# Norm 0's mean eleven ticks sooner, attention's turns and value products two ticks later

## Chip, core and metric

The kernel runs on one core of one Trainium2 chip. Its engines run side by side, each through its own list of instructions: TensorE (PE, with its weight loader PEld), VectorE (DVE), ScalarE (ACT), GpSimd (POOL) and SyncE (SP, which here only issues DMAs). The metric is the device time of one execution in microseconds (us), and lower is better. Single instructions are read from a trace that the hardware profiler took of one execution.

## What is computed

One step of a decoder layer for 1024 prompt tokens and 8 x 8 sample tokens (together T = 1088 columns), width 1024. Cut to the parts that matter here:

```python
proj = rmsnorm(x, norm1_g) @ w_in
q, k, v, glu_a, glu_b, gate_a, gate_b = jnp.split(proj, SPLIT_IDX, axis=-1)
attn = swa(q, k, v, sinks)                      # window 128, 16 heads, 4 key heads
branch_a = attn @ w_o_attn
c = dwconv_valid(glu_a * jax.nn.sigmoid(glu_b), conv_b_w, conv_b_bias)   # 31 taps
branch_b = jax.nn.silu(layernorm(c, ln_b_g, ln_b_b)) @ w_pb
merged = jax.nn.sigmoid(gate_a) * branch_a + jax.nn.sigmoid(gate_b) * branch_b
h = x + merged @ w_out
...
y = h + ffn(rmsnorm(h))                         # up, 3-tap convolution, silu gate, down
```

The layer norm needs, for each token, the mean over the 1024 channels, then the mean of the squares of the centred rows.

## The kernel before

All matrices are held as a high and a low part, so that one product of a weight tile with activations is three matmuls (`mm3`, lines 212 to 214). `stream` multiplies one weight (128 output rows) with all 1088 columns in chunks of 384, 384 and 320, eight inner steps for each chunk, and calls `tick` before each inner step. A **tick** is therefore one group of three products; one weight is 24 ticks.

Other work is woven into these streams. `plan` puts pairs of a due tick and a function on an agenda, sorted by due tick, and `tick` calls those that are due. The function then issues its instructions at this place of the program. The order in which an engine runs them isn't quite the program's: a planner, at build time, goes through all instructions with a model of their durations, and lets each engine take the one of highest priority (earlier in the program, unless `later` shifts it) among those whose inputs it believes ready. The order that comes out is fixed; on the chip each engine follows it and waits where an input isn't there.

**Attention** runs in two halves of the heads (`p` = 0 and 1), beside the streams of gates and convolution branches. A half has eight units of 128 query rows (`attn_unit`) and four sample units (`sample_unit`, steps at ticks 0, 12 and 18). `plan_units` lays units out at a spacing of 22 ticks (first half) or 19 (second), and 13 behind a sample unit; the order is two units, one sample unit, and so on. The first unit's steps that are due at `A_TURN[0]` or later wait for 10 or 16 ticks more. A unit handles two key heads, `g` = 0 and 1:

- `scores(g)` at `A_SCORE`: eight matmuls (L453, L454) into two PSUM banks, copies and masks (L456, L458), then the softmax: maximum (L418), four Exp on ACT (L420), reciprocal (L422), four normalisations on ACT (L424);
- `values()` at tick 8: high and low part of the values;
- `turn(g)` at `A_TURN`: four transposes of the softmax on PE (L465), then a cast on ACT (L247), a subtraction on DVE (L248) and, but for the first unit, a masked copy on DVE (L473), into single buffers `pt` and `pt0`;
- `mix(g)` at `A_MIX`: the product with the values (L484, two or four matmuls of 512 columns), a copy on ACT (L489) and an addition on DVE (L490); for `g` = 1 the result is split (L493, L494 and an accumulating DMA that POOL issues, L495), and in the first half it is written to memory ten ticks on (`attn_spill`).

`turn` moves its evictions 60 priority steps ahead when a branch gate (`gate_u`, Sigmoid, L772) was issued at most three ticks ago.

**The layer norm** over the convolution's output begins in the last of the gate streams (`LAST_GATES`) and goes on beside the attention's output projection (`do_o`). It has four parts (norm 0 to 3, 272 columns each), each with four steps (`ln_steps`) that are due at the ticks in `LN_AT`, counted from the start of the last gate stream: `load` (DMA, L637), `first` (sums over the channels on DVE, L623), `center` and `apply`. `center` issues a product with a matrix of 1/1024 (`mean`, L631, tied behind the last issued product of the streams), the subtraction of its result on DVE (L647), and for each half of the columns a square on ACT (L650) and three additions on DVE (L623). `apply` issues the second mean (L631 too), then square root, reciprocal (L387), scaling (L663) and Silu (L665). `do_o` loads a gate row (`ga`, L1069), runs a Sigmoid on it (L1070) and multiplies each chunk with it (L1074). Evictions of the gates are copies on ACT (L244).

Of the kernel before, what the change touches and what calls it, by code (L numbers as in the profile page):

```python
# [68 lines left out]
FACTOR_AFTER = 1  # L69
A_VALUES = 8  # L70
A_SCORE = (0, 5)
A_TURN = (16, 22)
A_MIX = (23, 29)
SPILL = 10
WEIGHTS_SOONER = -100
THIRD = 6
# [9 lines left out]
W_PARTS = 4  # L86
CONV_LATER = 1200
TURN_SOONER = -60
LN_AT = ((0, 0, 15, 36), (0, 37, 50, 80), (60, 81, 103, 134), (90, 135, 152, 183))
LEAD = (0, 0)  # L90
FIRST_UNIT = (10, 16)
SPACING = ({"u": 22, "s": 13}, {"u": 19, "s": 13})
# [40 lines left out]
class Build:  # L133
# [292 lines left out]
    def attn_unit(self, p, blk, st):  # L426
# [17 lines left out]
        def scores(g):  # L444
            pt = live[g]["pt"] = self.t(self.at, [P, 4, WIN + 4], "p", bufs=2)
            hd = 4 * (2 * p + g)
            nc.gpsimd.tensor_copy(pt[:, :, WIN:WIN + 1], self.c("sink", hd, 4)[:, :, None])
            above = self.masks[:, 0:WIN].bitcast(mybir.dt.uint32)[:, None, :]
            for jj in range(2):
                ps = self.bank("aux").rearrange("p (a b) -> p a b", a=2)  # L450
                for j in range(2):
                    h = 2 * jj + j
                    nc.tensor.matmul(ps[:, j, :], q[g][:, h, qs], kd[g][:, keys], start=True, stop=False)  # L453
                    nc.tensor.matmul(ps[:, j, :], q[g][:, h, qs], kl[g][:, keys], start=False, stop=True)  # L454
                two = pt[:, 2 * jj:2 * jj + 2, 0:WIN]
                nc.scalar.copy(two, ps[:, :, own])  # L456
                other = ps[:, :, 0:WIN] if blk else self.least[:, None, :].to_broadcast([P, 2, WIN])
                nc.vector.copy_predicated(two, above.to_broadcast([P, 2, WIN]), other)  # L458
            self.band_softmax(pt)

        def turn(g):
            pt = live[g]["pt"]
            ps = self.bank("aux")
            for h in range(4):
                nc.tensor.transpose(ps[:, h * P:(h + 1) * P], pt[:, h, 0:P], self.ident)  # L465
            x = self.t(self.at, [P, 2, 512], "pt", F32R)
            parts = [(0, x[:, y]) for y in range(2)]
            with self.later(TURN_SOONER if self.now - self.gated <= 3 else 0):
                self.split_ps(x[:, 0], x[:, 1], ps)
                if blk:  # L470
                    below = self.masks[:, None, WIN:2 * WIN].to_broadcast([P, 8, WIN])
                    x0 = self.t(self.at, [P, 2, 512], "pt0", F32R)
                    nc.vector.tensor_tensor(x0.rearrange("p y (a b) -> p (y a) b", a=4),  # L473
                                            x.bitcast(F32).rearrange("p y (a b) -> p (y a) b", a=4), below, ALU.mult)
                    parts += [(1, x0[:, y]) for y in range(2)]
            live[g]["parts"] = parts

        def mix(g):
            r, o = [slice(x * HD, (x + 1) * HD) for x in (g, 1 - g)]
            av = self.bank("aux")  # L480
            parts = live[g]["parts"]
            for n, (y, x) in enumerate(parts):
                v = vals["vt"][:, y, 2 * g:2 * g + 2, :].rearrange("p x d -> p (x d)")
                nc.tensor.matmul(av, v, x, start=n == 0, stop=n == len(parts) - 1)  # L484
            if g == 0:
                live[0]["t"] = self.t(self.at, [P, 4 * P], "av", bufs=2).rearrange("p (a b) -> p a b", a=4)
            t = live[0]["t"]
            av = av.rearrange("p (a b) -> p a b", a=4)
            nc.scalar.copy(t[r], av[o])  # L489
            nc.vector.tensor_tensor(t[r], av[r], t[r], ALU.add)  # L490
            if g == 1:
                h, l = q[0][:, :, qs], q[1][:, :, qs]
                nc.scalar.copy(h, t)  # L493
                nc.scalar.activation(l, h.bitcast(F32), AF.Identity, scale=-1.0)  # L494
                nc.gpsimd.dma_start(l, t, accum_op=ALU.add)  # L495
                if p == 0:
                    self.plan([(self.now + SPILL, lambda: self.attn_spill(st, qs))])

        steps = [(A_VALUES, values)]
        for g in range(2):  # L500
            steps.append((A_SCORE[g], lambda g=g: scores(g)))
            steps.append((A_TURN[g], lambda g=g: turn(g)))
            steps.append((A_MIX[g], lambda g=g: mix(g)))
        return steps
# [106 lines left out]
    def ln_steps(self, i):  # L611
# [46 lines left out]

        return [(at, f) for at, f in zip(LN_AT[i], (load, first, center, apply))]

# [72 lines left out]
    def phase_x(self):  # L733
# [152 lines left out]
        def plan_units(p):  # L886
# [5 lines left out]
            for kind, n in todo:  # L892
                new = self.attn_unit(p, n, st) if kind == "u" else self.sample_unit(p, n, st)
                wait = 0 if steps else FIRST_UNIT[p]
                steps += [(at + d + wait * (d >= A_TURN[0]), f) for d, f in new]
                at += SPACING[p][kind] + wait
# [1332 lines left out]
```

## Time and profile before

| What | us |
| --- | --- |
| median of three runs | 1634.8 |
| lowest and highest run | 1634.24, 1635.79 |
| the profiled execution | 1633.05 |
| its span, first to last instruction | 1631.3 |
| attention's first half beside the streams | 195 to 370 |
| attention's second half | 440 to 600 |
| last gate stream and norm | 600 to 720 |

A row of a timeline has the start (us from the start of the span), the duration, engine, line, operation and tiles (out<-in) and, in brackets, how long the engine was idle before it and what ended that. Rows of the waits view give who waited for whom, the total in us, how many times, and the longest. In a row of a group, the numbers are minimum, median and maximum in ns, then the first and last start.

### The profile page before, as it was taken

The page shows a single profiled execution, that of the slowest core. Times are in us where ns is not written, and L with a number is a line of the kernel's source. Part 1 is how long each engine was busy: PE and PEld are TensorE (multiplying, and loading weights), DVE is VectorE, ACT ScalarE, POOL GpSimd, SP SyncE. Part 2 cuts the span into 40 slices and gives each one's busy share as a digit, 9 for nine tenths or more (in the row PEclk, how much of TensorE's full clock was granted, in tenths as well). Part 3 has the DMA queues.
Part 4 walks back from the last instruction along what each step waited for, and adds up shares of the span by engine and source line. Part 5 has one row for each costly group of instructions (what it writes and reads, how often), then busy time and mean ns, then how long its engine had stood idle before and what let it go on. Part 6 is the DMA issues. An engine that isn't in the chain of part 4 may idle for free.

```text
span 1631.3 us, 30109 instructions
## 1 busy us (share of the span) xinstructions
PE 1618.2 (99%) x11428; PEld 1602.1 (98%) x11428; DVE 1341.7 (82%) x2395; ACT 911.4 (56%) x1964; POOL 316.2 (19%) x579
## 2 busy tenths in 40 slices
PE   9999999999999999999999999999999999999998
PEld 9999999999999999999999999999999999999997
DVE  7879678999999745788755999988888877989767
ACT  6536387885688755575533466555555555524232
POOL 0211122322132321121003442223232101000000
PEclk9999999999999999999999999999999999999999
DMA  6355455657646576648763532344444325766323
GB/s 212 106 127 129 97 133 117 139 112 154 150 93 130 127 192 227 197 149 219 194 229 101 200 119 84 112 119 115 120 115 117 100 100 163 236 165 160 108 62 110
DMA packets 130585, 229.90 MB, mean 141 GB/s; under 512 B 28552, under 2 KB 78728, under 8 KB 130424
## 3 DMA queue, kind: packets, MB, share of 16 engines
q1 hardware_dynamic: 94872, 140.13, 28.1%
q0 software_dynamic: 35136, 87.45, 23.2%
q8 instruction: 90, 1.47, 0.4%
q14 instruction: 55, 0.45, 0.1%
q10 hardware_dynamic: 432, 0.40, 0.1%
HBM read 157.47 MB, written 64.03 MB: 136 GB/s over the span
## 4 chain that ended last, share of the span: by engine, by line
PE 56%; DVE 2%; DMA 1%; issue 1%; ACT 1%; POOL 0%; POOLq 0%; DVEq 0%; ACTq 0%; SPq 0%
PE mm L212 12%; PE mm L213 12%; PE mm L214 12%; PE aux L214 6%; PE aux L212 6%; PE aux L213 6%; DMA d_ma<-ma 1%; ACT ct L665 0%; DMA ct<-d_c 0%; DMA wraw<-wall 0%; DMA d_t<-ct 0%; DVE ct L673 0%; ACT L665 0%; PE aux L1371 0%; DVE ct L647 0%
## 5 line engine op out<-in xcount | busy, mean ns | idle before, releaser
L212 PE MATMUL mm<-xh,whi 128*128 128x384 f32 (+1 forms) x904 | 299.6, 331 | 0.0
L213 PE MATMUL mm<-xl,whi 128*128 128x384 f32 (+1 forms) x904 | 296.0, 327 | 0.2 <-DVE xl L302 0.2
L214 PE MATMUL mm<-xh,wlo 128*128 128x384 f32 (+1 forms) x904 | 296.2, 328 | 0.0
L213 PEld LDWEIGHTS mm<-xl,whi 128*128 128x128 f32 x904 | 170.1, 188 | 2.4 <-DVE xl L302 0.7
L212 PEld LDWEIGHTS mm<-xh,whi 128*128 128x128 f32 x904 | 170.2, 188 | 1.8 <-ACT xh L301 0.3
L214 PEld LDWEIGHTS mm<-xh,wlo 128*128 128x128 f32 x904 | 169.9, 188 | 0.9 <-DMA wlo<-wall 0.3
L1475 DVE SCALAR_TENSOR_TENSOR acc<-st,fc,acc 128x1104 f32<-128x1104 f32 x88 | 119.9, 1366 | 12.2 <-issue 6.7
L214 PE MATMUL mm<-th,wlo 128*128 128x272 f32 x320 | 92.5, 290 | 0.0
L213 PE MATMUL mm<-tl,wlo 128*128 128x272 f32 x320 | 92.4, 289 | 0.0
L212 PE MATMUL mm<-th,wlo 128*128 128x272 f32 x320 | 92.3, 289 | 0.0
L585 DVE SCALAR_TENSOR_TENSOR bt<-u,consts,bt 128x513 f32<-128x513 f32 x120 | 89.6, 747 | 0.3
L585 DVE SCALAR_TENSOR_TENSOR c<-sm,hsum,c 128x512 f32<-128x512 f32 x120 | 89.4, 745 | 0.1
L214 PE MATMUL mm<-mh,wlo 128*128 128x272 f32 (+4 forms) x304 | 89.0, 293 | 0.0
L585 DVE SCALAR_TENSOR_TENSOR c<-u,consts,c 128x512 f32<-128x512 f32 x112 | 83.5, 746 | 0.3 <-ACT c L596 0.2
L247 ACT CAST whi<-wraw 128x512 fp32r<-128x512 f32 x76 | 47.5, 625 | 63.4 <-DVE wraw L1671 26.4
L1820 ACT COPY st<-mm 128x272 f32<-128x272 f32 (+2 forms) x132 | 43.7, 348 | 55.9 <-PE mm L214 55.9
L247 ACT CAST wlo<-wraw 128x512 fp32r<-128x512 f32 x76 | 47.4, 624 | 40.1 <-DVE wraw L1671 16.5
L1473 ACT ACTIVATE acc<-st,fc 128x1104 f32<-128x1104 f32 x44 | 57.6, 1316 | 15.1 <-DVE st L1776 11.8
L183 ACT CAST whi<-wraw 128x1024 fp32r<-128x1024 f32 x37 | 38.9, 1052 | 47.1 <-PE mm L213 46.0
L212 PE MATMUL aux<-mh,whi 128*128 128x272 f32 (+4 forms) x216 | 63.9, 296 | 0.0
L213 PE MATMUL aux<-ml,whi 128*128 128x272 f32 (+4 forms) x216 | 63.6, 294 | 0.0
L185 POOL DMA_DIRECT2D wlo<-wall x37 | 33.4, 902 | 150.5 <-ACT wlo L184 100.9
(723 smaller groups left out, 5839.1 us busy)
## 6 DMA issues: line engine op xcount, KB each, us to landing
wraw<-wall SPq DMA_DIRECT2D x118, 512.0 KB, 4.0
wlo<-wall POOLq DMA_DIRECT2D x37, 512.0 KB, 6.9
bw<-d_b SPq DMA_DIRECT2D x42, 272.0 KB, 4.0
d_b<-gd POOLq DMA_DIRECT2D x36, 272.0 KB, 6.1
d_b<-acc POOLq DMA_DIRECT2D x24, 272.0 KB, 4.7
ar<-wdn SPq DMA_DIRECT2D x32, 192.0 KB, 4.0
d_g<-acc POOLq DMA_DIRECT2D x10, 544.0 KB, 4.2
ct<-d_c SPq DMA_DIRECT2D x8, 544.0 KB, 6.2
```

The lines of the kernel that those rows point to most:

```text
L183: self.cast = self.nc.scalar.copy(h, r).ins
L185: self.nc.gpsimd.dma_start(l, self.a["wall"][i], accum_op=ALU.add)
L212: mm(ps, wh, xh, start=first, stop=False, skip_group_check=more)
L213: mm(ps, wh, xl, start=False, stop=False, skip_group_check=more)
L214: self.last_mm = mm(ps, wl, xh, start=False, stop=last, skip_group_check=more).ins
L247: self.cast = self.nc.scalar.copy(h, src).ins
L585: mac = lambda o, x, w: nc.vector.scalar_tensor_tensor(o, x, w, o, ALU.mult, ALU.add)
L1473: nc.scalar.activation(acc, st[:, 0:AW], AF.Identity, bias=fb(f), scale=fw(f, 0))
L1475: nc.vector.scalar_tensor_tensor(acc, st[:, k:k + AW], fw(f, k), acc, ALU.mult, ALU.add)
L1820: self.evicted = (add if second and n == 0 and j == 1 else op)(d, r(banks[bank, j]))
```

## The change

Three constants. Turns are due two ticks later behind the start of their unit, and so are the products with the values; scores, values and sample units keep their ticks, and so does the spacing of units. In the first norm part, `center` is due at tick 4 of the last gate stream and no longer at tick 15; `load`, `first` and `apply` stay.

```diff
-A_TURN = (16, 22)
-A_MIX = (23, 29)
+A_TURN = (18, 24)
+A_MIX = (25, 31)
...
-LN_AT = ((0, 0, 15, 36), (0, 37, 50, 80), (60, 81, 103, 134), (90, 135, 152, 183))
+LN_AT = ((0, 0, 4, 36), (0, 37, 50, 80), (60, 81, 103, 134), (90, 135, 152, 183))
```

## The prediction

> **What bounds the kernel now.** I read the page first, then the waits of TensorE (PE), then busy time by stage, then the timelines around each wait.
>
> ```profile
> span 1631.3 us, 30109 instructions
> ...
> PE 1618.2 (99%) x11428; PEld 1602.1 (98%) x11428; DVE 1341.7 (82%) x2395; ACT 911.4 (56%) x1964; POOL 316.2 (19%) x579
> ```
>
> PE is the bound: 13.1 us of 1631.3 are idle. The change removes no PE work, so it can win only idle time, and the places to look at are those that its steps touch. The busy time by stage has the columns stretch, length, then busy us of PE, weight load, DVE, ACT and POOL; the waits view has total, times, longest.
>
> ```profile
> 195.00:370.00 175.00, 173.74 (x1123) 169.23 (x1122) 155.82 (x288) 139.66 (x379) 49.65 (x75) 1.00 0.57 121
> 370.00:440.00 70.00, 70.00 (x429) 69.72 (x428) 68.83 (x113) 37.98 (x71) 10.24 (x16) 1.00 0.66 150
> 440.00:600.00 160.00, 159.15 (x1008) 154.07 (x1007) 133.22 (x257) 127.28 (x367) 46.80 (x69) 1.00 0.55 122
> 600.00:720.00 120.00, 117.63 (x706) 116.17 (x705) 78.67 (x106) 66.10 (x85) 20.44 (x35) 1.00 0.64 210
> ...
> PE aux L631 <- DVE sm L623: 2.4, 2, 2.0
> ...
> PE aux L465 <- ACT p L424: 1.0, 1, 1.0
> PE aux L484 <- DVE pt L248: 0.7, 2, 0.5
> ...
> PE aux L542 <- ACT ts L537: 0.2, 1, 0.2
> ```
>
> The two attention stretches (195 to 370 and 440 to 600) hold 1.26 + 0.85 = 2.1 us of idle PE, the norm stretch 2.4. That is all that the change can win there: 4.5 us, 0.28%. The norm's part is nearly one wait:
>
> ```profile
> 632.85 0.34 PE L213 MATMUL mm<-al,whi 128*128 128x384 f32 x1
> 633.02 0.34 PE L214 MATMUL mm<-ah,wlo 128*128 128x384 f32 x1
> 635.41 0.70 PE L631 MATMUL aux<-sm,mean 128*128 128x272 f32 x2 [2.05 <-DVE sm L623]
> ```
>
> The second mean of norm 0 (the variance, tick 36) waits for the sums of squares. Neighbouring products start 0.17 us apart (632.85, 633.02); here it is 2.39, so the wait costs 2.39 - 0.17 = 2.2 us.
>
> **Norm 0's mean, tick 15 to tick 4.** The chain that makes the sums late:
>
> ```profile
> 616.50 0.34 PE L214 MATMUL mm<-xh,wlo 128*128 128x384 f32 x1
> ...
> 622.39 0.62 PE L631 MATMUL aux<-sm,mean 128*128 128x272 f32 x2
> ...
> 605.39 0.30 DVE L623 TENSOR_TENSOR sm<-u 128x136 f32<-128x136 f32 x1
> ...
> 616.23 1.23 DVE L194 TENSOR_TENSOR wlo<-wraw,whi 128x1024 fp32r<-128x1024 f32 x1 [6.88 <-ACT whi L193]
> 623.05 2.42 DVE L647 TENSOR_TENSOR ct<-ct,aux 128x2176 f32<-128x2176 f32 x1 [5.60 <-PE aux L631]
> 630.65 1.20 DVE L623 TENSOR_TENSOR c<-c 128x544 f32<-128x544 f32 x2 [5.18 <-ACT c L650]
> 631.89 0.30 DVE L623 TENSOR_TENSOR sm<-c 128x136 f32<-128x136 f32 x1
> ...
> 633.73 1.20 DVE L623 TENSOR_TENSOR c<-c 128x544 f32<-128x544 f32 x2
> 634.96 0.30 DVE L623 TENSOR_TENSOR sm<-c 128x136 f32<-128x136 f32 x1
> ...
> 619.52 0.48 ACT L244 COPY gt<-mm 128x384 f32<-128x384 f32 x1 [3.00 <-PE mm L214]
> 626.83 1.28 ACT L1070 ACT_TABLE_LOAD   x1 [6.84 <-DMA ga<-d_ga]
> 628.13 1.12 ACT L1070 ACTIVATE ga<-ga 128x1088 f32<-128x1088 f32 x1
> 629.15 0.46 ACT L244 COPY gt<-mm 128x384 f32<-128x384 f32 x1
> 629.50 1.12 ACT L650 ACTIVATE c<-ct 128x1088 f32<-128x1088 f32 x1
> ```
>
> The centred rows are ready at 623.05 + 2.42 = 625.5, but the first square starts at 629.50: it stands on ACT behind the Sigmoid of the output gate (L1070), which waits 6.84 us for its DMA. So ACT's order makes the sums late. In the last gate stream tick 4 falls after the third group of three products, whose last one starts at 616.50: the mean starts near 616.7, 5.7 us sooner. It adds no PE wait, since its input is done at 605.69, 11 us before. What moves with it: two mean products (0.62), the subtraction (2.42), two squares (1.12 each), six additions (1.50 for each square); no DMA, so no queue of SP or POOL is passed. The subtraction follows L194 on DVE: 617.5 to 619.9. The first square then follows the eviction at 619.52, which the mean in front of it makes 0.6 later: 620.6 to 621.7. Adding up 1.50 with small gaps, the second square, and adding up again (1.1 + 1.5 + 1.1 + 1.5, from 620.6) ends at about 625.9. PE needs it at 633.2. Even if only the second square falls behind the Sigmoid, it starts at about 629.3 and the sums end at 631.9, still in time. Cost of the edit: nothing on PE; **gain 2.2 us**, unless both squares stay behind the Sigmoid. Then the gain is 0. I take 2.2: the planner put the Sigmoid between the evictions at 619.52 and 629.15, and the first square is now ready right behind the first of the two. Next late is the 0.35 that is left of L631's 2.4; I leave it.
>
> **Turns and value products, two ticks later.** A tick is three products, 3 x 0.174 = 0.52 us, so turns stand 1.04 us later behind their softmax. Turn to value product stays seven ticks. No instruction is added. The biggest wait is a turn's:
>
> ```profile
> 339.11 1.28 ACT L772 ACT_TABLE_LOAD   x1
> 340.40 1.06 ACT L772 ACTIVATE u<-u 128x1024 f32<-128x1024 f32 x1
> 341.37 1.26 ACT L424 ACTIVATE p<-p,den 128x128 f32<-128x128 f32 x4
> ...
> 341.80 0.33 PE L465 MATMUL aux<-consts,p 128*128 128x128 f32 x1 [1.03 <-ACT p L424]
> ...
> 467.36 0.73 PE L484 MATMUL aux<-pt,vt 128*128 128x512 f32 x2 [0.54 <-DVE pt L248]
> ```
>
> The turn at 341.80 waits for normalisations that stand on ACT behind the branch gate's table load and Sigmoid. Neither moves. If PE comes 1.04 later, the wait of 1.03 is gone. But counted in groups of products this turn (unit 6 of the first half, due tick 203) already stands two ticks behind its due place: the planner thought its input late. If it stands there again, nothing is won. The row lies between: I take 0.5 of 1.03. What is left of the second stretch's 0.85 beside L484's 0.7, 0.15, I count to the turns too, and all of it goes. Together 0.6. The value products' waits (0.7) and the sample unit's (0.2) hang on evictions and casts whose distance doesn't change; only their neighbours do. I take 0.2 of 0.9. **Sum 0.8 us**, with bounds: 2.1 if all idle time of both stretches goes, and below zero the crowding, next.
>
> What the later steps pass: a first-head value product issues evictions on ACT and DVE only; the second one's also the accumulating DMA on POOL (L495), and in the first half two spills on SP ten ticks on, each also two ticks later. The first half's last spill moves from tick 242 to 244 of the 264 before the second half's queries; the second half's last value product moves from 217 to 219 of 240, and the last sample unit stays behind it at 225. So nothing is cut off, and the loads that follow have room:
>
> ```profile
> 591.15 9.66 SPq L637 DMA_DIRECT2D ct<-d_c  x4
> 600.99 3.29 SPq L1026 DMA_DIRECT2D ah<-d_ah  x1
> ...
> 595.16 1.30 POOL L495 DMA_DIRECT2D q<-av  x1 [1.94 <-ACT q L494]
> ...
> 627.41 0.34 PE L212 MATMUL mm<-ah,whi 128*128 128x384 f32 x1
> ```
>
> If their buffers come free 1.04 us later, the norm's input is at 606.7 instead of 605.7 (needed at 616.7), and ah is issued 25 us before its use. That costs nothing. If this cover were gone, it would cost at most the 1.04. One turn (unit 1, due tick 50) now falls within three ticks of a branch gate and gets its eviction ahead of the gate; one eviction on ACT, inside idle time of ACT (139.66 of 175 busy).
>
> **A reading that gives more.** These rows bear on how much of PE's time is really waiting:
>
> ```profile
> L484 PEld LDWEIGHTS aux<-pt,vt x120: 186/188/228, 223.0 to 590.2; 128*128 128x128 f32 x120
> L484 PE MATMUL aux<-pt,vt x120: 387/395/504, 223.2 to 590.4; 128*128 128x512 f32 x120
> ```
>
> The weight loader is idle for 175 - 169.23 + 160 - 154.07 = 11.7 us in the two stretches, PE for 2.1. Were all of the 11.7 waiting that slack can remove, the gain would be 2.2 + 11.7 = 13.9 us: 1620.9, a rival. The rows speak against it: a value product lasts 395 ns over a load of 188, so its loader pauses although PE works. [...]
>
> **The sum.** -2.2 - 0.8 = -3.0. The profiled execution took 1633.05 us (span 1631.3 and 1.75 around it), so 1630.05 is its own forecast; on the median of 1634.8 it is **1631.8**.
>
> **The rivals.**
> - *The squares stay behind the Sigmoid.* For it: the planner did so before, and fills ACT whenever the gate's load seems landed. Against: the squares are now ready 5.6 us sooner. Time: 1634.8 - 0.8 = 1634.0. [...]
> - *Crowding, slower.* In eight pairs of neighbouring units (four in each half) the second turn now comes two ticks behind the next unit's first scores (spacing 22), or on the very tick of its second scores, with the value product one tick on (spacing 19). Their evictions and softmax meet on ACT and DVE, and the value product or the next turn waits. At the nearest row's 1.03 for each pair that is +8.2, less 2.2: 1640.8. It is slower than before from 0.28 us a pair, and measurably so from 0.68. Against it: the turns gain 1.04 of slack everywhere, and the dense places of before cost 0.5 at most (467.36).
> - *All waits go.* The norm's 2.2 and 0.35, and attention's 2.1: 1630.2.
> - *The change moves nothing that PE feels:* the planner sets every turn and the mean by its own idea of readiness. 1634.8. Against: nearly all turns stand on their due ticks now.
>
> **How the numbers follow.** Forecast 0.60, squares behind the Sigmoid 0.13, crowding 0.10, all waits gone 0.14, no effect 0.02, the weight loads' room 0.01. A difference of about 0.2%, 3.3 us, is what a measurement can tell here; that puts the border of faster at 1631.5, inside the forecast's own range of 1630.6 to 1633.4. Of its 0.60 I put 0.27 below the border, 0.32 within, 0.01 above. Faster: 0.27 + 0.14 + 0.01 = 0.42. Within: 0.32 + 0.13 + 0.02 = 0.47. Slower: 0.01 + 0.10 = 0.11. The range of 1629.9 to 1635.2 takes in the forecast, the Sigmoid case, all waits gone and a crowding of up to 0.3 a pair.
>
> **What would show it.** Norm 0's first mean near 616.7 without idle time before it; both squares ahead of L1070's table load on ACT; no wait of L631 at its second mean, and PE's idle time from 600 to 720 near 0.3. In attention the waits of L465 below 0.6 in all and PE's idle time in the two stretches near 1.3. The prediction is wrong if L650 still follows L1070, or if L465, L484 or L453 show waits of over 2.1 together.

## The result, and the profile after

The changed kernel took 1629.37 us (median of 9 runs, 1628.54 to 1633.16); the kernel before, run again beside it, 1634.24 us (9 runs, 1632.02 to 1635.79). The ratio is 0.9972, with a 95% interval of 0.9963 to 0.9981: faster by 3.1 to 6.0 us. The forecast was 1631.8 and its range ended at 1629.9, so the direction was right and the gain was sized too small. The profiled execution of the changed kernel took 1631.03 us, which is 2.1 us less than the profiled one of before (1633.05), not 4.9: single executions scatter by more than the parts of this change are worth, and that has to be kept in mind below.

The page of the changed kernel, span and busy time:

```profile
span 1629.2 us, 30104 instructions
...
PE 1618.2 (99%) x11428; PEld 1601.7 (98%) x11428; DVE 1342.4 (82%) x2395; ACT 910.8 (56%) x1964; POOL 320.5 (20%) x579
```

PE is busy for the same 1618.2 us as before; the 2.1 us are idle time that went. Where it went shows in busy time by stage (columns as in the prediction):

```profile
195.00:370.00 175.00, 174.95 (x1129) 170.35 (x1129) 156.35 (x289) 139.34 (x379) 47.83 (x75) 1.00 0.57 123
...
440.00:600.00 160.00, 159.16 (x1013) 154.90 (x1012) 132.63 (x257) 126.93 (x365) 51.09 (x70) 1.00 0.56 124
600.00:720.00 120.00, 118.12 (x704) 116.02 (x703) 79.22 (x107) 65.91 (x85) 19.87 (x34) 1.00 0.63 207
```

Attention's first half has 0.05 us of idle PE left, where it had 1.26. The second half still has 0.84, and the norm stretch 1.88 of its 2.37. The waits of PE say why:

```profile
PE aux L631 <- DVE sm L623: 1.7, 1, 1.7
...
PE aux L484 <- DVE pt L248: 0.8, 1, 0.8
```

No turn (L465) waits any more. L631 waits once, and it is another of its instances than before. Norm 0's two means on PE's timeline:

```profile
615.12 0.34 PE L214 MATMUL mm<-xh,wlo 128*128 128x384 f32 x1
615.29 0.62 PE L631 MATMUL aux<-sm,mean 128*128 128x272 f32 x2
...
631.64 0.34 PE L214 MATMUL mm<-ah,wlo 128*128 128x384 f32 x1
631.81 0.62 PE L631 MATMUL aux<-sm,mean 128*128 128x272 f32 x2
```

and the squares on ACT's:

```profile
618.55 1.11 ACT L650 ACTIVATE c<-ct 128x1088 f32<-128x1088 f32 x1 [3.42 <-DVE ct L647]
...
621.32 1.12 ACT L650 ACTIVATE c<-ct 128x1088 f32<-128x1088 f32 x1 [1.29 <-issue]
625.53 1.28 ACT L1070 ACT_TABLE_LOAD   x1 [3.10 <-DMA ga<-d_ga]
```

Both squares now stand ahead of the gate's Sigmoid (L1070), which still waits for its DMA. The second mean follows 0.17 us behind the product in front of it, so it does not wait at all. The wait that L631 has left belongs to norm 2's second mean; here is its row on PE, then DVE's timeline in front of it:

```profile
684.89 0.73 PE L631 MATMUL aux<-sm,mean 128*128 128x272 f32 x2 [1.75 <-DVE sm L623]
...
683.67 0.49 DVE L1074 TENSOR_TENSOR ma<-mm,ga 128x320 f32<-128x320 f32 x1 [2.60 <-DMA d_ma<-ma]
684.07 0.43 DVE L623 TENSOR_TENSOR c<-c 128x272 f32<-128x272 f32 x1
684.54 0.30 DVE L623 TENSOR_TENSOR sm<-c 128x136 f32<-128x136 f32 x1
```

The gated product (L1074) needs one of two buffers `ma`, whose store had not landed, and the norm's last two additions stand behind it.

In attention, what became of the turn that had waited longest (unit 6 of the first half) is on ACT:

```profile
337.69 1.28 ACT L424 ACTIVATE p<-p,den 128x128 f32<-128x128 f32 x4
339.00 1.28 ACT L772 ACT_TABLE_LOAD   x1
340.29 1.21 ACT L772 ACTIVATE u<-u 128x1024 f32<-128x1024 f32 x2
```

and on PE:

```profile
340.91 0.60 PE L465 MATMUL aux<-consts,p 128*128 128x128 f32 x4
```

Before, its four normalisations (L424) stood behind the branch gate's table load and Sigmoid and ended after 342. Now the list of ACT has them ahead, they end at 339.0, and the turn runs on its own due tick, in one piece and without a wait. Counted by products, the 16 turns of the first half stood in 34 pieces before (parts of the last three one to four ticks late, others broken up by products) and stand in 16 pieces now, each on its due tick.

### The profile page after: what moved, and what is told of

It is laid out like the page before. It is cut to its first block, busy times and chain, and to the rows that moved or that the text cites. A ratio compares the mean times of both kernels' runs of the same rounds, so it can differ in the third digit from the quotient of the medians.

```text
span 1629.2 us, 30104 instructions
## 1 busy us (share of the span) xinstructions
PE 1618.2 (99%) x11428; PEld 1601.7 (98%) x11428; DVE 1342.4 (82%) x2395; ACT 910.8 (56%) x1964; POOL 320.5 (20%) x579
## 4 chain that ended last, share of the span: by engine, by line
PE 86%; DVE 7%; DMA 3%; ACT 2%; issue 1%; SPq 0%; DVEq 0%; ACTq 0%; POOLq 0%
PE mm L212 20%; PE mm L213 20%; PE mm L214 20%; PE aux L212 7%; PE aux L213 7%; PE aux L214 7%; DVE c L585 2%; PE aux L484 2%; ACT ct L665 1%; DMA q<-ql 1%; DVE bt L585 1%; PE aux L465 1%; PE aux L453 1%; PE aux L454 1%; DMA ct<-d_c 1%
## 5 line engine op out<-in xcount | busy, mean ns | idle before, releaser
L212 PEld LDWEIGHTS mm<-xh,whi 128*128 128x128 f32 x904 | 170.1, 188 | 1.8 <-ACT xh L301 0.5
```

The lines of the kernel that those rows point to most:

```text
L212: mm(ps, wh, xh, start=first, stop=False, skip_group_check=more)
```

## The experiments

A measure that doesn't depend on what the page calls busy helps to read them. All traces have the same 10,680 products of lines 212 to 214. The table has, for each profiled execution, the time to the start of the 1,201st product (attention begins), and then on to the 2,001st (its first half), the 3,001st (its second half), the 3,601st (norm 0 to norm 2), the 4,601st (next) and the end of the span (rest). The kernel before was profiled four times in all, the changed kernel twice.

| us | to attention | first half | second half | norm | next | rest | span |
| --- | --- | --- | --- | --- | --- | --- | --- |
| before, in the prediction | 200.6 | 176.6 | 207.4 | 107.6 | 136.0 | 803.0 | 1631.3 |
| before_a | 200.2 | 176.7 | 207.2 | 108.5 | 137.7 | 802.1 | 1632.3 |
| before_b | 201.1 | 176.5 | 207.4 | 109.3 | 136.8 | 802.1 | 1633.2 |
| before_c | 200.6 | 176.2 | 207.3 | 108.5 | 137.9 | 802.1 | 1632.7 |
| changed | 200.6 | 175.4 | 207.2 | 107.3 | 136.6 | 802.1 | 1629.2 |
| both_again | 200.5 | 175.4 | 206.4 | 105.8 | 136.8 | 802.1 | 1626.9 |
| norm_alone | 202.9 | 175.4 | 207.1 | 106.2 | 136.4 | 802.1 | 1630.1 |
| turns_alone | 200.7 | 175.4 | 206.2 | 108.3 | 137.5 | 802.1 | 1630.1 |
| norm2_later | 200.7 | 175.4 | 206.5 | 104.7 | 137.5 | 802.9 | 1627.8 |
| centre_10 | 200.9 | 175.4 | 206.0 | 110.1 | 136.4 | 802.1 | 1630.9 |
| third_buffer | 200.5 | 175.4 | 206.0 | 104.9 | 142.3 | 802.4 | 1631.4 |
| turns_4 | 200.5 | 174.6 | 206.2 | 106.5 | 135.4 | 802.4 | 1625.6 |
| turns_sooner | 200.9 | 178.8 | 206.8 | 105.7 | 139.4 | 803.4 | 1635.0 |
| three_together | 200.5 | 174.7 | 206.6 | 104.8 | 142.4 | 802.5 | 1631.5 |

The mean of the four rows of before and the mean of the two of the changed kernel differ by 1.1 us in attention's first half (176.5 and 175.4), 0.5 in the second (207.3 and 206.8), 2.0 in the norm (108.5 and 106.5) and 0.4 in the next stage, most of which the change doesn't touch; the spans by 4.3 (1632.4 and 1628.1).

**both_again**: the changed kernel, unaltered.

> The changed kernel once more, profiled and timed. Theory A (norm 2's second mean waits by chance, for a store that lands late in some executions): the same 4 to 5 us faster than before as in the first timing, and in the new trace the wait of L631 is anything from 0.3 to 1.8 us, not 1.75 again. Theory B (the norm's gain is given back there each time): the wait is 1.75 again within 0.2, and the gain stays 4 to 5 us although the profiled spans differ by 2.1 only, which B can't explain.

Measured: 1628.97 us (6 runs), ratio 0.9971, interval 0.9960 to 0.9983. The gain repeats. The wait at norm 2's second mean was 0.79 us here and 1.75 in the first profile of the same kernel, so its size is a matter of the execution, as theory A has it.

**norm_alone** and **turns_alone**: one part each.

```diff
 norm_alone, against the changed kernel
-A_TURN = (18, 24)
-A_MIX = (25, 31)
+A_TURN = (16, 22)
+A_MIX = (23, 29)
 turns_alone, against the changed kernel
-LN_AT = ((0, 0, 4, 36), ...
+LN_AT = ((0, 0, 15, 36), ...
```

> Only the first norm's mean at tick 4, turns and value products at their old ticks. Theory A: 2.2 us faster than before (ratio 0.9987), both squares ahead of the gate's Sigmoid on ACT, no wait of L631 at its second mean; attention's waits of before (L465 1.0, L484 0.7) stay. Theory B: the same at the second mean, but 1.4 of it come back as a longer wait at norm 2's second mean: 0.5 to 0.8 us faster. Theory C (the two edits act on each other through the planner's order): neither, under 0.3 us.

> Only the turns and value products two ticks later, the norm's mean back at tick 15. Theory A: 1.4 to 2.4 us faster than before, L465 without a wait, the wait of 2.05 of L631 at norm 0's second mean still there. Theory B: 3.5 to 4 us faster, most of the whole. My prediction's size for this part was 0.8.

Measured, beside a kernel before of 1634.27: norm_alone 1631.41, ratio 0.9984 (0.9976 to 0.9993), turns_alone 1632.89, ratio 0.9992 (0.9983 to 1.0000). That is 2.9 us (1.1 to 3.9) and 1.4 us (0 to 2.8), 4.2 together, against 5.3 for both in the same comparison; the intervals are over 1 us wide to each side, so the parts add as far as this can tell. The waits of turns_alone:

```profile
PE aux L631 <- DVE sm L623: 3.1, 2, 2.2
```

The 2.2 at norm 0's second mean is back without the norm's edit, and there is no row of L465. So each edit removes the wait that it was aimed at, and not the other's. Norm 2's wait was 0.90 in turns_alone and 1.16 in norm_alone; it isn't a price of the norm's edit alone.

The table has one surprise: norm_alone's first half takes 175.4 us like that of the changed kernel, though its turns stand at their old ticks. The norm's edit can't be why: up to 610 us PE, ACT and DVE have the same lists as in before, with unit 6's normalisations behind the gate's Sigmoid. But PE, which had reached attention 2.3 us late (it waited 1.0 us near 9, and 1.1 near 180 for a DMA), came to that turn 2.1 us later than in the first profile of before, and the normalisations only 1.2 us later (342.54 and 341.37), so the turn waited 0.13. The whole 1.1 us fall between the 1,801st and the 1,861st product, around this unit's turns. So that is where the first half of before loses this time, and a PE that comes later against ACT gets it back too.

**norm2_later**: is norm 2's wait worth removing by a later second mean?

```diff
-(60, 81, 103, 134)
+(60, 81, 103, 138)
```

> The changed kernel with norm 2's second mean four ticks later (tick 138, not 134), so 2.1 us more room where the changed kernel waited 1.75. Theory A: the wait is gone from the profile, the median gains 0 to 0.7 us over the changed kernel, as the wait is long in few executions only. Theory B: 1.7 us faster than the changed kernel.

Measured: 1631.18, ratio 0.9984 (0.9975 to 0.9993), some 2 us slower than the changed kernel in the same comparison, where theory A forecast a gain of up to 0.7 and theory B one of 1.7. Norm 2's wait is gone from its profile, but norm 3's second mean waits in its place:

```profile
706.87 0.34 PE L214 MATMUL mm<-q,wlo 128*128 128x384 f32 x1
709.12 0.72 PE L631 MATMUL aux<-sm,mean 128*128 128x272 f32 x2 [1.91 <-DVE sm L623]
```

The later step pushes its scaling and Silu into the next part's squares: the Silus start 2.2 us later than in both_again's profile (694.67 and 692.43) and norm 3's second square 1.9 us later (706.04 and 704.10). This profile is of the fastest of its eleven executions (1629.60), so it doesn't show where the 2 us of the median went.

**centre_10**: is it the sooner mean, or the place of the squares on ACT?

```diff
-LN_AT = ((0, 0, 4, 36), ...
+LN_AT = ((0, 0, 10, 36), ...
```

> The changed kernel with norm 0's centring at tick 10 instead of 4 (before it was 15). At tick 10 the list of ACT puts both squares (L650) behind the output gate's Sigmoid (L1070) again, although their mean is still five ticks sooner than before. Theory D (the place of the squares on ACT, ahead of the Sigmoid that waits for its gate row, is what the norm's gain comes from): PE waits again about 2 us (1.5 to 2.5) at norm 0's second mean near 631, the first square again starts right behind the Sigmoid, and the time is that of the turns alone, 1632.9 (1631.8 to 1633.9), or 1631.1 at least. Rival E (a sooner mean is enough, wherever the squares stand): no wait there of over 0.4, and the time of the changed kernel, 1629.2 (1628.2 to 1630.2).

Measured: 1632.59, ratio 0.9997 (0.9988 to 1.0006); nothing is left of the norm's gain. ACT in that profile:

```profile
617.24 0.48 ACT L244 COPY gt<-mm 128x384 f32<-128x384 f32 x1 [3.00 <-PE mm L214]
624.40 1.28 ACT L1070 ACT_TABLE_LOAD   x1 [6.68 <-DMA ga<-d_ga]
625.69 1.11 ACT L1070 ACTIVATE ga<-ga 128x1088 f32<-128x1088 f32 x1
626.71 1.10 ACT L650 ACTIVATE c<-ct 128x1088 f32<-128x1088 f32 x1
```

The subtraction ended at 620.6 (618.17 + 2.42, on DVE), the first square could have run then, and it runs at 626.71, because the Sigmoid stands first and waits for its DMA until 624.40. Theory D holds, and rival E falls: what counts is on which side of the waiting Sigmoid the squares stand. And PE pays more than the wait:

```profile
632.97 0.77 PE L631 MATMUL aux<-sm,mean 128*128 128x272 f32 x2 [1.89 <-DVE sm L623]
633.30 0.75 PE L212 MATMUL mm<-ah,whi 128*128 128x384 f32 x1
633.85 0.52 PE L213 MATMUL mm<-al,whi 128*128 128x384 f32 x1
634.17 0.52 PE L214 MATMUL mm<-ah,wlo 128*128 128x384 f32 x1
```

Behind the wait the products take 0.52 us and start 0.32 apart, where they take 0.34 and start 0.17 apart elsewhere. From the mean on, 40 PE instructions take 8.09 us instead of 6.51. In windows of 5 us from 630 the granted clock is 0.85 and 0.81 and then 1.00 again; as an estimate from these shares, with the clock either whole or half, it was halved for (0.15 + 0.19) x 5 / 0.5 = 3.4 us.

**before_a, before_b, before_c**: does that also happen in the kernel before? Three more profiles of it, one execution each.

> The kernel before, looked at again. In centre_10 PE idled 1.89 us at norm 0's second mean, and then its products started 0.32 us apart instead of 0.17 for some 3 us: the granted clock was halved, and 40 PE instructions took 8.09 us instead of 6.5. In the first profile of before the wait there was 2.05 us and the clock stayed whole. Theory L (the norm's gain measured 2.9 instead of 2.2 because in some executions of before this wait also halves the clock, at about 1.6 us more): in one or two of three profiles of before the 40 instructions behind the wait take about 8 us, and those executions are the longer ones. Rival M (it doesn't happen at that place in before; the 0.7 is noise of the medians): 6.5 us in all three. The turn's wait near 341 was 1.03 in the first profile and 0.1 with the same order in norm_alone: I expect 0 to 1.1, so not the same each time.

> As before_a: the second of three profiles of before. Theory L: in one or two of the three the 40 PE instructions behind norm 0's second mean take about 8 us; rival M: 6.5 in all. The wait itself 1.9 to 2.3 in each.

> As before_a: the third of three profiles of before. Theory L: in one or two of the three the 40 PE instructions behind norm 0's second mean take about 8 us; rival M: 6.5 in all. The wait itself 1.9 to 2.3 in each.

Measured: 1634.05, 1634.93 and 1634.47 us. Norm 0's second mean on PE in before_a:

```profile
634.93 0.70 PE L631 MATMUL aux<-sm,mean 128*128 128x272 f32 x2 [2.06 <-DVE sm L623]
```

in before_b:

```profile
636.50 0.70 PE L631 MATMUL aux<-sm,mean 128*128 128x272 f32 x2 [2.79 <-DVE sm L623]
```

and in before_c, with two of the products behind it:

```profile
634.87 0.70 PE L631 MATMUL aux<-sm,mean 128*128 128x272 f32 x2 [1.96 <-DVE sm L623]
...
636.21 0.52 PE L213 MATMUL mm<-q,whi 128*128 128x384 f32 x1
636.53 0.52 PE L214 MATMUL mm<-q,wlo 128*128 128x384 f32 x1
```

and before_c's granted clock by stretch (the column before the last two):

```profile
636.00:638.00 2.00, 2.00 (x8) 2.00 (x7) 1.97 (x2) 0.10 (x1) 0.03 (x1) 0.50 0.64 258
```

In before_c the clock was halved behind the wait (0.50 from 636 to 638): 40 instructions took 8.07 us. In before_a and before_b they took 6.51, although before_b's wait was the longest of all. So theory L holds for one profile in four. Its second half, that such executions are the longer ones, fell: before_b, without the drop, took 1634.93. The turn's wait was 1.03, 1.03 and 0.9 us, as it was in the first profile; only norm_alone, whose first 200 us had 2 us of other waits, showed 0.13.

**third_buffer**: norm 2's wait removed at its root.

```diff
-r = self.t(self.lt, [P, 384], "ma", bufs=2)
+r = self.t(self.lt, [P, 384], "ma", bufs=3)
```

> The changed kernel with three buffers for the gated products (ma, L1074) instead of two. PE's list stays the same. Theory F (norm 2's second mean waits because the product L1074 in front of the last two additions on DVE waits for a buffer whose store to memory hasn't landed): DVE's idle time in front of L1074 near 682 to 685 is below 0.3 (2.60 in the changed kernel's profile), L631's wait there is below 0.3 (1.75, 0.79, 1.16 and 0.90 in four profiles), and the time is 0.8 to 1.8 below the changed kernel's 1629.2: 1627.4 to 1628.4. Rival G (another input of that mean, or of the next, is as late): L631 or its neighbours wait as long as before, and the time stays 1629.2 (1628.4 to 1630).

Measured: 1632.87, ratio 0.9995 (0.9987 to 1.0004), which is 3 us and more above the changed kernel. Theory F names the right cause: the product in front of the last two additions no longer waits, and norm 2's second mean (681.20) follows its neighbour at once. But its time is wrong, and rival G's "or of the next" came true, more strongly than G put it. DVE's list has changed, and norm 3's first mean waits for its last addition, which now stands behind two long instructions of norm 2 (L387 and L663). Its load had also landed late: the second pair of additions could start at 687.62, and at 685.09 in both_again. DVE's timeline:

```profile
687.62 0.72 DVE L623 TENSOR_TENSOR u<-ct 128x544 f32<-128x544 f32 x1 [0.57 <-DMA ct<-d_c]
...
688.73 1.84 DVE L387 RECIPROCAL bt<-bt 128x272 f32<-128x272 f32 x1
...
690.78 2.41 DVE L663 TENSOR_TENSOR ct<-ct,bt 128x2176 f32<-128x2176 f32 x1
693.11 0.29 DVE L623 TENSOR_TENSOR sm<-u 128x136 f32<-128x136 f32 x1
```

and PE's:

```profile
690.24 0.34 PE L214 MATMUL mm<-q,wlo 128*128 128x384 f32 x1
693.55 1.25 PE L631 MATMUL aux<-sm,mean 128*128 128x272 f32 x2 [2.97 <-DVE sm L623]
...
695.23 0.52 PE L214 MATMUL mm<-q,wlo 128*128 128x384 f32 x1
```

The wait costs 2.97, and the halved clock behind it (0.50 granted from 694 to 698) another 3.1 (40 instructions in 9.58 us instead of 6.5). In the table the stage has 142.3 instead of 136.7.

**turns_4** and **turns_sooner**: how much of attention is slack behind the softmax?

```diff
 turns_4, against the changed kernel
-A_TURN = (18, 24)
-A_MIX = (25, 31)
+A_TURN = (20, 26)
+A_MIX = (27, 33)
 turns_sooner, against the changed kernel
-A_TURN = (18, 24)
-A_MIX = (25, 31)
+A_TURN = (14, 20)
+A_MIX = (21, 27)
```

> The changed kernel with turns and value products four ticks later than before (20, 26 and 27, 33) instead of two. Theory H (the gain of attention is slack of the turns behind their softmax; two ticks already take all of L465's waits): waits of L465 stay at 0, L484's 0.4 to 0.8, time 1629.2 (1628.2 to 1630.2). Rival I (more slack frees more, since waits are hidden in PE's busy time): another 1 us or more below, 1628.2 or less. Rival J (crowding: the second turn now comes on or past the next unit's scores): waits of L465, L484 and L453 together over 2, time 1631.2 or more.

> The changed kernel with turns and value products two ticks sooner than before (14, 20 and 21, 27), so four sooner than in the change. Theory H (slack behind the softmax): the turns come 2.1 us sooner than in the changed kernel, so waits of L465 appear at several of the 32 turns, 3 us or more in all, and the time is 1633 or more. Rival K (attention's distances hardly matter, the 1.4 us of the turns alone are scatter): waits of L465 below 1, time 1629 to 1631.

Measured, beside a kernel before of 1632.99: turns_4 1627.73 (5 runs), ratio 0.9968 (0.9956 to 0.9981); turns_sooner 1635.58 (11 runs), ratio 1.0009 (1.0000 to 1.0019), which gives the norm's gain back. Attention's first half, busy time by stage, in turns_4:

```profile
195.00:370.00 175.00, 175.00 (x1135) 171.11 (x1134) 155.84 (x290) 140.94 (x380) 51.14 (x75) 1.00 0.56 124
```

and in turns_sooner:

```profile
195.00:370.00 175.00, 173.57 (x1108) 166.33 (x1108) 153.88 (x285) 135.72 (x372) 46.45 (x72) 1.00 0.54 119
```

Kernel by kernel, from two ticks sooner to four later, the first half takes 178.8, 176.5, 175.4 and 174.6 us. PE's idle time there is 1.43, 1.26, 0.05 and 0, the weight loader's 8.67, 5.77, 4.65 and 3.89. From the change to turns_4 the stage gains another 0.8 us although PE was hardly idle any more, and turns_sooner loses 2.3 against before with only 0.17 more idle time and 1.4 us of waits of L465, where theory H wanted 3 or more; its time came out as theory H had it, and rival K fell. So part of the waiting does not show as idle PE. That the loader's idle time falls with the stage's time is arithmetic: from the 1,201st to the 2,001st product the loader is busy for 170.1 to 170.9 us in all fourteen profiles, and the rest of the stage is its idle time. PE counts as busy for 177.4 us of that stretch in turns_sooner and 174.6 in turns_4, for the same products. Rival I's direction is right on that stage, with 0.8 us where it wanted 1 or more. On the whole kernel turns_4's ratio isn't told apart from the change's 0.9972. turns_4 doesn't show the crowding of rival J.

In turns_4 unit 6's normalisations stand behind the gate's Sigmoid again, and the turn still doesn't wait. ACT, then PE:

```profile
337.91 1.28 ACT L772 ACT_TABLE_LOAD   x1
339.21 1.06 ACT L772 ACTIVATE u<-u 128x1024 f32<-128x1024 f32 x1
340.18 1.26 ACT L424 ACTIVATE p<-p,den 128x128 f32<-128x128 f32 x4
...
341.22 0.61 PE L465 MATMUL aux<-consts,p 128*128 128x128 f32 x4
```

The gate's table load starts 1.2 us sooner than in before (339.11), and the turn comes late enough. So the other order on ACT is one way to take this wait away, and not the only one.

**three_together**: turns_4, the third buffer, and norm 3's first mean six ticks later.

```diff
-A_TURN = (18, 24)
-A_MIX = (25, 31)
-(90, 135, 152, 183)
-r = self.t(self.lt, [P, 384], "ma", bufs=2)
+A_TURN = (20, 26)
+A_MIX = (27, 33)
+(90, 135, 158, 183)
+r = self.t(self.lt, [P, 384], "ma", bufs=3)
```

> Turns and value products four ticks later, three buffers for the gated products, and norm 3's first mean six ticks later (158 instead of 152), since in third_buffer that mean waited 2.97 us for sums behind a late load and then ran at half clock. Theory F with that mended: no wait of L631 over 0.5 from 600 to 720, no halved clock, time 0.6 to 1.6 below turns_4: a ratio to before of 0.9958 to 0.9965, about 1626.5 to 1627.5. Rival G (the wait moves on once more, to norm 2's scaling, norm 3's second mean or the first products of the last stage): L631 or L1233's rows wait 1 us or more, ratio 0.9968 or above.

Measured: 1633.71, ratio 0.9997 (0.9988 to 1.0006), which is what rival G forecast: norm 3's second mean now waits.

```profile
709.67 0.73 PE L631 MATMUL aux<-sm,mean 128*128 128x272 f32 x2 [2.69 <-DVE sm L623]
710.03 0.54 PE L212 MATMUL mm<-q,whi 128*128 128x384 f32 x1
710.41 0.47 PE L213 MATMUL mm<-q,whi 128*128 128x384 f32 x1
710.67 0.53 PE L214 MATMUL mm<-q,wlo 128*128 128x384 f32 x1
```

The clock is low behind it again (0.62 and 0.53 granted in the two windows of 2 us from 710, 8.06 us for 40 instructions). The four norm parts share ACT and DVE, and in these runs each repair but the first moved the wait to the next part or step. No version here is shown to beat the changed kernel.

## Why the prediction was right and where it failed

**Norm 0: the mechanism right, the size not refuted.** The mean ran at 615.29 without idle time; both squares stand ahead of L1070's table load (the first even ahead of the eviction that the prediction put in front of it); the sums end at 624.0 (623.70 + 0.30 on DVE), where 625.9 was worked out; and the second mean, needed at 631.8, doesn't wait. centre_10 shows that the order on ACT decides: its first square, ready at 620.6, started behind the Sigmoid at 626.71. The term was 2.2; norm_alone measured 2.9 by the clock (1.1 to 3.9), and the norm's stage fell by 2.3 in norm_alone and by 2.0 in the changed kernel, so 2.2 stands. That is partly luck, since two things that the term left out seem to cancel. It priced one execution's wait by its length. In four profiles of before the waits were 2.05, 2.06, 2.79 and 1.96, 2.2 on average; the second mean's start lies another 0.17 behind, as in the prediction's working; and behind one of the four the clock was halved, for 1.56 more. That makes 2.2 + 0.2 + 1.56/4 = 2.8 us. Against it stands the next wait.

**"Next late is the 0.35 that is left of L631's 2.4."** It was the right place, but 0.35 was one draw: norm 2's wait was 0.3, 0.9, 1.1 and 0 us in four profiles of before, 0.6 on average, and 1.75 and 0.79 in two of the changed kernel. That is why PE's idle time from 600 to 720, which the prediction put near 0.3, was 1.88. Its cause is the store of `ma` (third_buffer). Whether the norm's edit makes it longer on average is open; six profiles don't say.

**Attention: the step that failed.** The prediction said of the normalisations behind the gate's Sigmoid, "Neither moves", reckoned with a PE that comes 1.04 us later, feared that the planner would set the turn late again, and took 0.5 of 1.03. These steps were wrong. In the profiles with the two ticks the normalisations moved ahead of the gate's table load on ACT, the turn stood on its due tick, and the whole wait went; in the two with four ticks it went too, in the old order. Nor did PE come later: in before nine groups of products lay between the two turns of unit 6, where six were due, so the turn stood three ticks late (the prediction counted two); now it is six, and the turn stands one group sooner in PE's list than before. The first half alone gained 1.1 us and the second 0.5 (0.1 in the first profile of the changed kernel, 0.7 to 1.3 in all others with its turns or later ones), 1.6 against the 0.8 of the sum. By the clock turns_alone gained 1.4, with an interval from 0 to 2.8, so the times alone don't refute 0.8; the traces do, by the steps above. What the second half's gain is made of is open, and so is why the planner chose the other order on ACT.

**The rivals.** *The squares behind the Sigmoid* did not happen at tick 4; at tick 10 it does. *Crowding* isn't seen at two ticks or at four. *All waits go* (1630.2) came nearest of the times that were given, but its account isn't what happened: the turns' waits went, while norm 2's and L484's 0.8 stayed. *The weight loads' room* was wrong as a time, 1620.9. Over the four settings of the turns the stage's time fell by 4.2 us and PE's idle time by 1.4, so idle PE doesn't show all of the waiting. But the loader's idle level was no forecast either: of its 11.7 us in the two stretches 9.75 are still there in the changed kernel's first profile, and how much of that could go no run shows.

**The base.** The forecast stood on a median of 1634.8 from three runs. The same kernel had medians of 1634.24, 1634.27, 1632.99 and 1633.96 in later comparisons, so some tenths of a us of the miss are the base's: of the 2.4 us between 1631.8 and 1629.4, 0.6 are. By the profiles attention's term is 0.8 of it, and another 0.4 lie in the next stage, where the wait for DVE's L1233, 0.4 or 1.2 us in either kernel, changes from execution to execution. The remainder isn't located.

## What to carry to other kernels

Where an engine keeps its order, look at what an instruction stands behind and not only at when its input is ready: five ticks sooner on the wrong side of the Sigmoid were worth nothing, eleven on the right side 2.9 us. Where several chains share two engines, the first repair pays and the next ones may only move the wait, so look for what is late next before you repair a second time. Price a wait by several profiles of the kernel before, and give its tail a chance of its own: with the halved clock, the mean cost of norm 0's wait over four executions was a quarter above the one row that the forecast used. Look for the wait that stands in for it as well, as norm 2's did.

## What the runs showed of the hardware that was not expected

The granted clock of PE was halved behind some of its waits and not behind others. It was halved behind waits of 1.89 (centre_10), 1.96 (before_c), 2.69 (three_together) and 2.97 us (third_buffer), and was not behind waits of 1.75 (the changed kernel), 1.91 (norm2_later), 2.05 (before), 2.06 (before_a), 2.16 (turns_alone) and 2.79 (before_b). By the granted clock in windows, reckoned as for centre_10, it was halved for 3.4 us in the first three cases and for 6.8 in third_buffer. It cost 1.6 us in three cases and 3.1 us in the one of 2.97. So the length of the wait doesn't decide alone, and the same wait of one program costs 2 us in one execution (2.05 in before) and 3.5 in another (1.96 and 1.56 in before_c). No run was made to try what else decides, and why third_buffer's halved stretch lasted twice as long is open.
